# A hybrid attention and mLSTM layer: the scan stage of the last head by itself, its tiles laid out anew, stores on ScalarE's queue

## The chip, the cores and the metric

The kernel is one program on one NeuronCore of a Trainium2 chip. The time is device microseconds (us) of one execution. TensorE is called PE here, VectorE DVE, ScalarE ACT, GpSimd POOL and SyncE SP. SP computes nothing; it issues most of the DMAs, in the order in which they are written, and an issue that has to wait holds up everything behind it in that queue. ACT issues a few DMAs in the same way, between its own instructions. [...]

## The reference

One layer over 1152 tokens, 128 prompt tokens (block 0) and 1024 sample tokens (blocks 1 to 8), float32, width 1024:

```
h = rmsnorm(x) * (1 + sc1) + sh1                # adaLN from silu(cond) @ w_ada + b_ada, six parts
aq, ak, av, mq, mk, mv, mo, mg = split(h @ w_in)
attn_o = attention(rope(norm(aq)), keys, vals)  # 8 query heads of 64, 2 key heads, softmax over up to 1152 keys
hm     = mlstm_bidir(mq, mk, mv, mg)            # 4 heads of 128, chunks of 128, forward and backward scan
hm     = rmsnorm(hm) * sigmoid(mo)
x = x + g1 * (concat(attn_o, hm) @ w_out)       # w_out: 1024 x 1024
h2 = rmsnorm(x) * (1 + sc2) + sh2
x = x + g2 * ((silu(h2 @ w_g) * (h2 @ w_u)) @ w_down)   # inner width 2816
y = rmsnorm(x)
```

g1 is part 2 of the six adaLN parts, g2 part 5. The keys and values of the prompt and the scans' final states are returned too.

## The kernel before

Tokens come in nine blocks of 128 and three chunks of three blocks. Most float32 products are made of three: an operand is split into a high part (a rounded copy, by ACT) and the rest (by DVE or POOL), and high x high, high x rest and rest x high are added. `load_piece` (L139 to L153) does so for a weight: a DMA into a raw tile, ACT's copy at L152, DVE's subtraction at L137.

The program is a chain of stages. First come the projections, head by head; the scan of head h-1 and the attention of chunk 0 run beside the projection of head h. The change is in what follows:

- **The scan stage.** The scan of the last mLSTM head (`head_mlstm`, L822 to L900) has no projection beside it. For each block it makes weights (L843 to L851), products with the state (L866, L869) and with the values (L873), a sum on DVE (L876 to L884), and the block's output tile `hm` (L886 to L890). After blocks 2, 5 and 8 the last three blocks are normalised (DVE's `rsqrt`, L127 to L133, then POOL at L896) and stored to DRAM (`hm_d`, L898). Beside it run three others, advanced in turn by `weave` and `beside`: `ada`, which makes part 5 of the adaLN vector out of eight slices of w_ada (L341, L422, L441 to L454); `first`, which multiplies the attention output of chunk 0 by the upper half of w_out (`out_block`, L1148 to L1150, twelve matmuls for each block and each half of the columns, so 72), gates it (L1247) and adds it to x (POOL, L1248), storing the sums `x1a` at L1251; and `att`, the attention of chunk 1 (`attention`, L993 to L1074: scores S at L1036, softmax L1038 to L1043, two DMA transposes of the probabilities at L1045 and L1046, products with the values at L1060 and L1061).
- **The prefill** (`prefill`, L1150 to L1209). The pools of the scan stage are closed, and new pools take their memory. For each block it loads the scan's output from `hm_d` (L1162), transposes it on PE (L116), splits it (L1185 and L137), multiplies it by the lower half of w_out, and gates and adds. The loaded tile and the temporary of the gating share one tag, `t2`, with three buffers. The rows of chunk 0 are then normalised for the FFN (`norm2`). Units of `att` are put between the steps, 0.35 of one for each step.
- **The FFN** by chunks (L1316 to L1318 and L1116 to L1118), with the rest of `att` beside that of chunk 0.

Tiles of closed pools hand on their memory: the first DMA into a new tile waits for the last use of whatever lay there. The loop that begins with the tag `cs` at L527 names the tags of the pool `mlp` once, and so fixes their order in memory. The Tile framework's scheduler then orders the instructions of each engine when the program is built; `hot(n)` raises the priority of what stands under it.

Of the kernel before, what the change touches and what calls it, by code (L numbers as in the profile page):

```python
# [19 lines left out]
P = 128  # L20
# [25 lines left out]
def hybrid_step(ctx: ExitStack, tc: tile.TileContext, I: dict, O: dict):  # L46
# [11 lines left out]
    def nm(s):  # L58
        uid[0] += 1
        return f"{s}_{uid[0]}"  # L60
# [10 lines left out]
    def emit(gen):  # L71
        for _ in gen:
            pass
# [340 lines left out]
    Gv = G.rearrange("p t (d x) -> p d t x", d=2)  # L414


    def ada_rest(ns, silp, new_a4, new_part, new_row, early=2, whole=False):

        def rows_of(n, j, q, half):
            a4 = new_a4()  # L420
            lo = n * D + j * 512 + q * 256
            dma(a4, w_ada[half * 512 : half * 512 + 512, lo : lo + 256].rearrange("(k p) n -> p k n", p=P))  # L422
            return a4

        units = [(n, j, q, half) for n in ns for j in range(2) for q in range(2) for half in range(2)]
        ahead = [rows_of(*u) for u in units[:early]]
        for u, (n, j, q, half) in enumerate(units):
            if u + early < len(units):
                ahead.append(rows_of(*units[u + early]))
# [20 lines left out]
            mm(pr[0:2, :], strip_sel, part, start=True, stop=True)  # L450
# [76 lines left out]
    for tag, shape, bufs, dt in (("cs", [P, P + 1], CSB, F32), ("c0f", [P, P + 1], 2, F32), ("c0b", [P, P + 1], 1, F32), ("hm", [P, NB, P], 2, F32), ("ssh", [P, NB], 2, F32), ("nu", [P, 2, P + 1], 4, F32),  # L527
                                 ("it", [P, 2, P + 1], 3, F32), ("dn", [P, 2], 3, F32), ("jkh", [P, P], 1, BF16), ("sd", [P, 2, P], 4, F32),
                                 ("dt", [P, 2, P], 4, F32), ("so", [P, P], 9, F32), ("va", [P, P + 1], 9, F32), ("kT", [P, P], 9, F32),
                                 ("th", [P, P], 1, F32), ("qTm", [P, CT], 2 * NCH, F32), ("wv", [P, 2, P + 1], 2, F32), ("kt", [P, P], 2, F32)):  # L530
        mlp.tile(shape, dt, name=f"lay_{tag}", tag=tag, bufs=bufs)


# [565 lines left out]
    def t2():  # L1099
        return ft.tile([P, 512], F32, name=nm("t2"), tag="t2", bufs=3)  # L1100
# [20 lines left out]
            for ps, i in zip(banks, grp):  # L1121
                done(i, ps)

    def out_pieces(half, own=None):
        ws = []
        for n in range(2):
            pieces = []
            for j in range(2):
                r0 = half * 512 + 2 * j * P
                rows = w_out[r0 : r0 + 2 * P, n * 512 : (n + 1) * 512].rearrange("(a p) n -> p a n", p=P)  # L1130
                pieces.append(load_piece([(full_view, rows)], (2, 512), raw=own and own[2], own=own))
                own = None
            ws.append(pieces)
        return ws

    def out_gates():
        gs = []
# [15 lines left out]
    def prefill(cur, nxt):  # L1153

        x1s = cur["x1"], nxt["x1"]
        cur["rs"] = []

        def load_hm(b):
            if b == NB:
                return None  # L1160
            hm = t2()
            dma(hm, hm_d[b // CB][b % CB * P : (b % CB + 1) * P, :])  # L1162
# [10 lines left out]
        gx_all = xp.tile([P, D], F32, name="gx_all")  # L1173
        dma(gx_all, g_d[0, 0:1, :].to_broadcast([P, D]))
        gx = [gx_all[:, n * 512 : (n + 1) * 512] for n in range(2)]
        for b in range(NB):
            load_x1(b + 1)
            t = xp.tile([P, NQ, P], F32R, name=nm("mx"), tag="mx", bufs=2)
            th, tl = t[:, 0:4], t[:, 4:8]
            hm, ahead = ahead, load_hm(b + 1)  # L1180
# [4 lines left out]
            nc.scalar.copy(th, psv)  # L1185
            sub(tl, psv, th.bitcast(F32), "dve")
            yield
            c, i = divmod(b, CB)
            for n in range(2):
                cs = slice(n * 512, (n + 1) * 512)  # L1190
                ps = out_block(ws, n, th, tl)
                g = gx[n] if b == 0 else gs[n]
                if c < 2:
                    add_gated(x1s[c][i], ps, g, n, pool)
                else:
                    xt = t2()
                    dma(xt, xrow(b)[:, cs])
                    t = t2()
                    dve.tensor_tensor(out=t, in0=ps, in1=g, op=ALU.mult)
                    pool.tensor_tensor(out=xt, in0=xt, in1=t, op=ALU.add)  # L1200
                    dma(x1_d[i][:, cs], xt)
                yield
            if c == 0:
                with hot(200):
                    cur["rs"] += stats(x1s[0][i : i + 1])
            if 0 < b <= CB:
                yield from norm2(0, cur, b - 1)

    def attn_out_first(oT, ready):  # L1209


        x1 = hTp.tile([P, CB, D], F32, name="x1a", tag="hT0")
        gt = hTp.tile([P, 6, 512], F32, name="gta", tag="hT1")
        mx = hTp.tile([P, CB, NQ, P], F32R, name="mxa", tag="hT2")
        ip = [wp.tile([P, 1024], F32R if i < 2 else F32, name=nm("ip"), tag="ipair", bufs=4) for i in range(4)]
        ir = [wp.tile([P, 1024], F32R if i < 2 else F32, name=nm("ir"), tag="iraw", bufs=4) for i in range(4)]
        turn = [0]

        def a4():
            turn[0] += 1  # L1220
            return ip[2 + turn[0] % 2].rearrange("p (k n) -> p k n", k=4)

        ada = ada_rest((5,), padded_sil(gt[:, 5, 0:256].rearrange("p (k c) -> p k c", k=KD)), a4,
                       lambda: ir[3][:, 0:512], lambda: ir[3][0:2, 512:1024], 1)

        def out():
            for n in range(2):
                cs = slice(n * 512, (n + 1) * 512)
                ws = []
                for j in range(2):  # L1230
                    rows = w_out[2 * j * P : (2 * j + 2) * P, cs].rearrange("(a p) n -> p a n", p=P)
                    ws.append(load_piece([(full_view, rows)], (2, 512), raw=ir[2], own=(ip[j], ir[j])))
                for cnd in range(2):
                    dma(gt[:, 2 * n + cnd], g_d[0, cnd : cnd + 1, cs].to_broadcast([P, 512]))
                yield
                for i in range(CB):
# [11 lines left out]
                    pool.tensor_tensor(out=v, in0=v, in1=gt[:, 4], op=ALU.add)  # L1248
                    yield
                    if n == 1:  # L1250
                        dma(x1a_d[i], x1[:, i])  # L1251

        return out(), ada

    def attn_out(a, oT, gs):

        ws = out_pieces(0)
        x1 = a["x1"]
        for i in range(CB):
            if i != 1:  # L1260
# [178 lines left out]
    es1.close()  # L1439
    es_wp.close()  # L1440
    es_d.close()
# [10 lines left out]
    cur["x1"], nxt["x1"] = new_x1(0), new_x1(1)  # L1452
    es_x = ExitStack()
    xp = es_x.enter_context(tc.tile_pool(name="xp", bufs=1, side="right", reuse_waits="tile"))
    due = 0.0
    for _ in prefill(cur, nxt):
        due += 0.35
# [103 lines left out]
```

## Time and profile before

| | |
|---|---|
| time, three runs | 1567.03 us median (1566.90 to 1569.09) |
| the profiled execution's own time | 1570.49 us, of which the span is 1568.7 us |
| PE busy | 1486.6 us, 95% of the span |
| DVE busy | 1014.5 us, 65% |
| ACT busy | 771.1 us, 49% |
| POOL busy | 268.4 us, 17% |
| mean granted PE clock | 0.981 of full speed |

Starts and durations below are microseconds from the start of the span. In a timeline a row gives start, duration, engine, line, operation, and out<-in; `xN` is a number of merged instructions, and a bracket holds the idle time of the engine before it and who ended it. A matmul's duration includes its way through the array; the distance from one start to the next says more of its cost. In a table by windows the columns are the window, its length, and for each engine the busy time and (xN) the number of instructions, then the granted PE clock, the share of the DMA engines that was busy and the GB/s moved.

### The profile page before, as it was taken

The numbers are of one execution on the slowest core, as the hardware profiler recorded it, in microseconds if no ns is written. First come the engines' busy times: TensorE is split into PE (matmuls) and PEld (weight loads), VectorE is DVE, ScalarE is ACT, GpSimd is POOL, SyncE is SP. The second block draws the span as 40 slices with busy tenths as digits, with TensorE's granted clock in tenths as the row PEclk, the third lists the DMA queues.
The fourth block names the chain that finished last, engine by engine and source line by source line (L and its number), as shares of the span: only waits on it lengthen the run. The fifth ranks groups of instructions, "written<-read, shape, count | busy, mean of one in ns | idle before, by whom it ended". The sixth has DMA issues, their size and how long they took to land. (4 is left out here: it accounts for less than half of the span.)

```text
span 1568.7 us, 23368 instructions
## 1 busy us (share of the span) xinstructions
PE 1486.6 (95%) x8539; PEld 1246.3 (79%) x8539; DVE 1014.5 (65%) x2009; ACT 771.1 (49%) x1413; POOL 268.4 (17%) x352
## 2 busy tenths in 40 slices
PE   6899999999999589999999999999999999999997
PEld 3545567677766468898998989989898989999996
DVE  4877555837659576677555676878866585554554
ACT  4754466847656344545432444556552443323333
POOL 0212423322343242100110101000010101001110
PEclk9899999999999799999999999999999999999999
DMA  9664423523646738768554446878773545534441
GB/s 363 189 188 152 89 69 41 118 50 68 127 141 167 259 79 199 184 182 174 149 154 148 148 127 223 200 173 183 173 172 114 165 131 175 161 117 139 148 139 63
DMA packets 387881, 236.91 MB, mean 151 GB/s; under 512 B 170198, under 2 KB 346790, under 8 KB 387766
## 3 DMA queue, kind: packets, MB, share of 16 engines
q1 hardware_dynamic: 385110, 231.84, 54.8%
q10 hardware_dynamic: 2656, 3.58, 1.1%
q8 instruction: 67, 1.10, 0.3%
q14 instruction: 48, 0.39, 0.1%
HBM read 183.79 MB, written 13.26 MB: 126 GB/s over the span
## 5 line engine op out<-in xcount | busy, mean ns | idle before, releaser
L152 ACT CAST whi<-raw 128x1024 fp32r<-128x1024 f32 (+1 forms) x216 | 221.8, 1027 | 410.0 <-PE mm L1317 154.4
L137 DVE TENSOR_TENSOR wlo<-raw,whi 128x1024 fp32r<-128x1024 f32 (+1 forms) x216 | 259.4, 1201 | 205.3 <-ACT whi L152 204.9
L1317 PE MATMUL mm<-aTl,whi 128*128 128x384 f32 x1056 | 355.7, 337 | 2.7 <-DVE aTl L137 2.7
L1318 PE MATMUL mm<-aTh,wlo 128*128 128x384 f32 x1056 | 354.3, 336 | 0.0
L1316 PE MATMUL mm<-aTh,whi 128*128 128x384 f32 x1056 | 353.5, 336 | 0.0
L137 POOL TENSOR_TENSOR hl<-tn,hl 128x384 fp32r<-128x384 f32 x66 | 85.3, 1292 | 839.7 <-ACT hl L1339 764.2
L1317 PEld LDWEIGHTS mm<-aTl,whi 128*128 128x128 f32 x1056 | 198.5, 188 | 3.9 <-DVE aTl L137 3.3
L1316 PEld LDWEIGHTS mm<-aTh,whi 128*128 128x128 f32 x1056 | 198.1, 188 | 0.6
L1318 PEld LDWEIGHTS mm<-aTh,wlo 128*128 128x128 f32 x1056 | 198.4, 188 | 0.0
L1117 PE MATMUL mm<-wlo,hl 128*128 128x512 f32 x372 | 145.7, 392 | 0.0
L1116 PE MATMUL mm<-whi,hl 128*128 128x512 f32 x372 | 144.4, 392 | 0.2 <-ACT hl L1339 0.2
L1118 PE MATMUL mm<-whi,hl 128*128 128x512 f32 x372 | 143.7, 393 | 0.3 <-POOL hl L137 0.3
L483 PE MATMUL wi<-ipair,hT 128*128 128x384 f16 (+2 forms) x408 | 134.9, 333 | 3.7 <-ACT th L760 1.3
L484 PE MATMUL wi<-ipair,hT 128*128 128x384 f16 (+2 forms) x408 | 134.8, 333 | 0.0
L485 PE MATMUL wi<-ipair,hT 128*128 128x384 f16 (+2 forms) x408 | 131.3, 333 | 2.0 <-DVE hT L137 2.0
L1043 DVE SCALAR_TENSOR_TENSOR pl<-pr,st,ph 128x1152 f16<-128x1152 f32 (+1 forms) x72 | 94.6, 1314 | 34.1 <-ACT ph L1042 33.2
L1039 ACT ACTIVATE pr<-S,st 128x1152 f32<-128x1152 f32 (+1 forms) x72 | 81.4, 1130 | 34.9 <-DVE st L1038 34.5
L1038 DVE TENSOR_REDUCE st<-S 128x1 f32<-128x1152 f32 (+1 forms) x72 | 88.8, 1233 | 14.0 <-PE S L1036 13.5
L1042 ACT ACTIVATE ph<-pr,st 128x1152 f16<-128x1152 f32 (+1 forms) x72 | 83.8, 1164 | 24.0 <-issue 11.1
L1036 PE MATMUL S<-kst,qT 128*128 128x384 f32 (+1 forms) x400 | 88.2, 350 | 1.8 <-ACT pr L1039 1.8
L1105 DVE TENSOR_TENSOR t<-mm,gl 128x512 f32<-128x512 f32 x102 | 68.9, 684 | 26.7 <-DMA gl<-g_d 10.3
L1118 PEld LDWEIGHTS mm<-whi,hl 128*128 128x128 f32 x372 | 69.9, 188 | 14.9 <-POOL hl L137 0.7
(381 smaller groups left out, 2525.5 us busy)
## 6 DMA issues: line engine op xcount, KB each, us to landing
raw<-in_w_gu_dram SPq DMA_DIRECT2D x132, 512.0 KB
raw<-in_w_down_dram SPq DMA_DIRECT2D x60, 512.0 KB
a<-in_w_ada_dram SPq DMA_DIRECT2D x24, 512.0 KB
gl<-g_d SPq DMA_DIRECT2D x36, 256.0 KB
aw<-in_w_ada_dram SPq DMA_DIRECT2D x16, 512.0 KB
iraw<-in_w_in_dram SPq DMA_DIRECT2D x32, 256.0 KB
raw<-in_w_out_dram SPq DMA_DIRECT2D x12, 512.0 KB
x<-in_x_sample_dram SPq DMA_DIRECT2D x11, 512.0 KB
```

The lines of the kernel that those rows point to most:

```text
L137: (dve if eng == "dve" else pool).tensor_tensor(out=out, in0=full, in1=hi, op=ALU.subtract)
L152: nc.scalar.copy(hi[:, :n], raw[:, :n])
L483: mm(ps[:, :n], ah, wh[:, k % 2, c0 : c0 + n], start=(k == 0), stop=False)
L484: mm(ps[:, :n], ah, wl[:, k % 2, c0 : c0 + n], start=False, stop=False)
L485: mm(ps[:, :n], al, wh[:, k % 2, c0 : c0 + n], start=False, stop=(k == KD - 1))
L1043: dve.scalar_tensor_tensor(out=plv, in0=prv, scalar=st[:, 3:4], in1=phv, op0=ALU.mult, op1=ALU.subtract)
L1116: mm(ps, ah, wh[:, k % 2, :], start=(k == 0), stop=False)
L1117: mm(ps, ah, wl[:, k % 2, :], start=False, stop=False)
L1118: mm(ps, al, wh[:, k % 2, :], start=False, stop=(k == nk - 1))
L1316: mm(ps, wh[:, k, :], th[:, k, :], start=(k == 0), stop=False)
L1317: mm(ps, wh[:, k, :], tl[:, k, :], start=False, stop=False)
L1318: mm(ps, wl[:, k, :], th[:, k, :], start=False, stop=(k == KD - 1))
```

## The change

Five things, all about the scan stage and the prefill:

1. **The attention goes behind the scan stage.** `attention(0)` is finished before the stage (`emit(att)`), and `attention(1)` first runs in the prefill. The rates of the other two go up: `ada` from 0.5 to 0.8 of a step for each step of the scan, `first` from 0.35 to 0.55.
2. **Layout.** The tags of `mlp` are named in another order. `x1a` and the split attention output `mxa` change places in the memory of the projection's input; the split halves of w_out's upper half lie in the `iraw` tiles, and their raw loads have two `ipair` tiles in place of one raw tile.
3. **The gate row of `ada`** lies in the scan's second output tile (`hmx`, tag `hm`), and its stores go by ACT's queue.
4. **The stores of `x1a`** are gathered and written out after the loops, on ACT's queue.
5. **The prefill** loads the scan's output into tiles of its own (`hmr`, two buffers), has three buffers for the split, splits blocks 0 and 1 first, and makes the left halves of both before the right ones. The second half of the lower w_out, and two loads of x, are issued behind the load of the gate.

```
@@ the layout of mlp
-    for tag, ... in (("cs", ...), ("c0f", ...), ("c0b", ...), ("hm", ...), ... ("qTm", ...), ("wv", ...), ("kt", ...)):
+    for tag, ... in (("hm", ...), ("ssh", ...), ("nu", ...), ... ("kt", ...), ("wv", ...), ("c0f", ...), ("c0b", ...),
+                     ("cs", [P, P + 1], CSB, F32), ("qTm", [P, CT], 2 * NCH, F32)):
@@ ada_rest
-            dma(g_d[0 if n == 2 else 1, :, j * 512 : (j + 1) * 512], row)
+            store(g_d[0 if n == 2 else 1, :, j * 512 : (j + 1) * 512], row)
@@ prefill
-            hm = t2()
+            hm = xp.tile([P, 512], F32, name=nm("hmr"), tag="hmr", bufs=2)
...
-        ahead = load_hm(0)
-        load_x1(0)
-        ws = out_pieces(1)
+        hms = [load_hm(0), load_hm(1)]
+        ws = [out_pieces(1, 0)]
         gs = out_gates()
+        with tc.issue_after(dma(gx_all, g_d[0, 0:1, :].to_broadcast([P, D])).ins):
+            load_x1(0)
+            load_x1(1)
+            ws.append(out_pieces(1, 1))
...
+        for b in range(2):
+            mix(b)
+            yield
+        for b in range(2):
+            half(b, 0)
+            yield
+        for b in range(2):
+            load_x1(b + 2)
+            half(b, 1)
+            yield
+            yield from end(b)
+        for b in range(2, NB):
+            load_x1(b + 2)
+            mix(b)
+            yield
+            for n in range(2):
+                half(b, n)
+                yield
+            yield from end(b)
@@ attn_out_first
-        x1 = hTp.tile(..., name="x1a", tag="hT0")
-        mx = hTp.tile(..., name="mxa", tag="hT2")
+        x1 = hTp.tile(..., name="x1a", tag="hT2")
+        mx = hTp.tile(..., name="mxa", tag="hT0")
+        his, los, raws = ir[0:2], ir[2:4], ip[2:4]
+        hmx = mlp.tile([P, NB, P], F32, name="hmx", tag="hm", bufs=2).rearrange("p b n -> p (b n)")
...
-                    ws.append(load_piece([(full_view, rows)], (2, 512), raw=ir[2], own=(ip[j], ir[j])))
+                    ws.append(load_piece([(full_view, rows)], (2, 512), raw=raws[j], own=(his[j], los[j])))
...
-                        dma(x1a_d[i], x1[:, i])
+                        stores.append((x1a_d[i], x1[:, i]))
@@ the stage
-    first, ada = attn_out_first(oT, done)
+    stores = []
+    first, ada = attn_out_first(oT, done, stores)
+    emit(att)
     oT = []
-    att = chain(att, attention(1, oT, set()))
-    weave(scan, beside((ada, 0.5), (first, 0.35), (att, 0.14)), 37, 37)
-    while len(done) < CB:
-        next(att)
+    att = attention(1, oT, set())
+    weave(scan, beside((ada, 0.8), (first, 0.55)), 37, 37)
     emit(first)
     emit(ada)
     emit(scan)
+    for out, v in stores:
+        nc.scalar.dma_start(out, v)
```

What this does to the instructions of an engine is the scheduler's doing. Two places carry the prediction.

PE at the end of the scan stage, before. `mxa` is the split attention output, `ip` and `ir` are the split w_out; `S` are scores; `po` and `vs` are the attention's product with the values.

```order
L1148 MATMUL mm_6214<-ip_5710,mxa 128x512
L1149 MATMUL mm_6214<-ir_5714,mxa 128x512
L1150 MATMUL mm_6214<-ip_5710,mxa 128x512
L450 MATMUL mm_6298<-ir_5716,strip_sel 2x512
L1036 MATMUL S_6581<-kst_1029,qT_5827 128x384 x6
L1060 LDWEIGHTS vs
L1060 MATMUL po_6412<-phT_5944,vs 128x256
L1061 LDWEIGHTS vs
L1061 MATMUL po_6412<-plT_5945,vs 128x256
```

The same place of the changed kernel; `wi<-va,sd` is the scan's product with the values, `wi<-cs,qT` that with the state, `hmr` the scan's output loaded back, `whi` and `wlo` the lower half of w_out, `mx` the split `hmr`.

```order
L450 MATMUL mm_6103<-hmx,strip_sel 2x512
L874 MATMUL wi_6158<-va_5591,sd_6017 128x129 x2
L867 MATMUL wi_6172<-cs_5608,qT_4895 128x129
L867 MATMUL wi_6172<-c_905_4693,qT_4895 128x129
L874 MATMUL wi_6178<-va_5687,sd_6081 128x129 x2
L116 MATMUL mm_6284<-ident,hmr_6247 128x128 x4
L116 MATMUL mm_6294<-ident,hmr_6249 128x128 x4
L1145 MATMUL mm_6303<-whi_6252,mx_6283 128x512
L116 MATMUL mm_6322<-ident,qr_6319 128x128 x4
L1146 MATMUL mm_6303<-wlo_6253,mx_6283 128x512
L1147 MATMUL mm_6303<-whi_6252,mx_6283 128x512
```

Between the scan's last product and the prefill's first transposes stood the last twelve matmuls of `first`, one set of scores and two sets of products with the values; now nothing stands there, and the attention's first transposes (`qr`) come inside the prefill. Counted over the whole order, 40 sets of scores (one head of one block each) stood ahead of the FFN's first matmul, 33 of them ahead of the prefill's first product; now it is 35 and 27. The products with the values come in sets of 18 matmuls for two heads: ahead of the prefill's first product stand two sets fewer than before, and in the prefill four where there were three.

SP's queue before, ahead of the first load of scan output:

```order
L1045 DMA_TRANSPOSE phT_6173<-ph_6256 128x9x128
L1251 DMA x1a_d_80<-x1a 128x1024
L1046 DMA_TRANSPOSE plT_6174<-pl_6257 128x9x128
L1251 DMA x1a_d_81<-x1a 128x1024
L454 DMA g_d<-ir_5716 2x512
L1045 DMA_TRANSPOSE phT_6497<-ph_6500 128x9x128
L1046 DMA_TRANSPOSE plT_6498<-pl_6501 128x9x128
L151 DMA raw_6338<-in_w_out_dram 128x2x512
L151 DMA raw_6344<-in_w_out_dram 128x2x512
L151 DMA raw_6350<-in_w_out_dram 128x2x512
L1162 DMA t_1279_6335<-hm_d_75 128x512
```

And in the changed kernel, where the two `ip` are the last slices of w_ada for `ada`:

```order
L422 DMA ip_5710<-in_w_ada_dram 128x4x256
L422 DMA ip_5709<-in_w_ada_dram 128x4x256
L151 DMA raw_6251<-in_w_out_dram 128x2x512
L151 DMA raw_6257<-in_w_out_dram 128x2x512
L1159 DMA hmr_6247<-hm_d_75 128x512
L1159 DMA hmr_6249<-hm_d_75 128x512
L1137 DMA gl_6263<-g_d 128x512
L1137 DMA gl_6265<-g_d 128x512
L1170 DMA gx_all<-g_d 128x1024
L1164 DMA x_1250_6239<-x1a_d_79 128x1024
L1164 DMA x_1250_6239<-x1a_d_80 128x1024
L151 DMA raw_6271<-in_w_out_dram 128x2x512
```

The stores of `x1a` and of the gate row and the transposes are gone from between, two weight loads stand ahead of the first load of `hmr`, and the other two behind the load of the gate. [...]

More of the change, by code (lines that the diff above doesn't have):

```diff
@@ L414, in hybrid_step, with ada_rest @@
     Gv = G.rearrange("p t (d x) -> p d t x", d=2)
-    def ada_rest(ns, silp, new_a4, new_part, new_row, early=2, whole=False):
+    def ada_rest(ns, silp, new_a4, new_part, new_row, early=2, whole=False, store=dma):
         def rows_of(n, j, q, half):
@@ L1122, in three_blocks, with out_pieces @@
                 done(i, ps)
[L1124 to L1134, printed above, removed]
+    def out_pieces(half, n):
+        pieces = []
+        for j in range(2):
+            r0 = half * 512 + 2 * j * P
+            rows = w_out[r0 : r0 + 2 * P, n * 512 : (n + 1) * 512].rearrange("(a p) n -> p a n", p=P)
+            pieces.append(load_piece([(full_view, rows)], (2, 512)))
+        return pieces
     def out_gates():
@@ L1186, in prefill, with half @@
             sub(tl, psv, th.bitcast(F32), "dve")
-            yield
+            hms.append(load_hm(b + 2))
+        def half(b, n):
             c, i = divmod(b, CB)
[L1189 to L1202, printed above, removed]
@@ L1203, in prefill @@
-            if c == 0:
+            cs = slice(n * 512, (n + 1) * 512)
+            ps = out_block(ws, n, *mixed[b])
+            g = gx[n] if b == 0 else gs[n]
+            if c < 2:
+                add_gated(x1s[c][i], ps, g, n, pool)
+            else:
+                xt = t2()
+                dma(xt, xrow(b)[:, cs])
+                t = t2()
+                dve.tensor_tensor(out=t, in0=ps, in1=g, op=ALU.mult)
+                pool.tensor_tensor(out=xt, in0=xt, in1=t, op=ALU.add)
+                dma(x1_d[i][:, cs], xt)
@@ L1204, in prefill, with end @@
+        def end(b):
+            if b < CB:
                 with hot(200):
-                    cur["rs"] += stats(x1s[0][i : i + 1])
+                    cur["rs"] += stats(x1s[0][b : b + 1])
             if 0 < b <= CB:
                 yield from norm2(0, cur, b - 1)
-    def attn_out_first(oT, ready):
-        x1 = hTp.tile([P, CB, D], F32, name="x1a", tag="hT0")
-        gt = hTp.tile([P, 6, 512], F32, name="gta", tag="hT1")
-        mx = hTp.tile([P, CB, NQ, P], F32R, name="mxa", tag="hT2")
-        ip = [wp.tile([P, 1024], F32R if i < 2 else F32, name=nm("ip"), tag="ipair", bufs=4) for i in range(4)]
-        ir = [wp.tile([P, 1024], F32R if i < 2 else F32, name=nm("ir"), tag="iraw", bufs=4) for i in range(4)]
+        for b in range(2):
+            mix(b)
+            yield
@@ new lines, in prefill, with attn_out_first @@
+        for b in range(2):
[14 more added lines that the diff above has]
+            yield from end(b)
+    def attn_out_first(oT, ready, stores):
+        x1 = hTp.tile([P, CB, D], F32, name="x1a", tag="hT2")
+        gt = hTp.tile([P, 6, 512], F32, name="gta", tag="hT1")
+        mx = hTp.tile([P, CB, NQ, P], F32R, name="mxa", tag="hT0")
+        ip = [wp.tile([P, 1024], F32, name=nm("ip"), tag="ipair", bufs=4) for i in range(4)]
+        ir = [wp.tile([P, 1024], F32R, name=nm("ir"), tag="iraw", bufs=4) for i in range(4)]
+        his, los, raws = ir[0:2], ir[2:4], ip[2:4]
+        hmx = mlp.tile([P, NB, P], F32, name="hmx", tag="hm", bufs=2).rearrange("p b n -> p (b n)")
@@ L1250, in out @@
                     if n == 1:
-                        dma(x1a_d[i], x1[:, i])
+                        stores.append((x1a_d[i], x1[:, i]))
         return out(), ada
     def attn_out(a, oT, gs):
-        ws = out_pieces(0)
+        ws = [out_pieces(0, n) for n in range(2)]
         x1 = a["x1"]
@@ L1454, in hybrid_step @@
     xp = es_x.enter_context(tc.tile_pool(name="xp", bufs=1, side="right", reuse_waits="tile"))
+    for tag, shape, bufs, dt in (("gx_all", [P, D], 1, F32), ("hmr", [P, 512], 2, F32), ("mx", [P, NQ, P], 3, F32R)):
+        xp.tile(shape, dt, name=f"lay_{tag}", tag=tag, bufs=bufs)
     due = 0.0
```

27 lines of the change are left out of this document (13 added, 14 removed).

## The prediction

> **What bounds the kernel now.** The summary of busy time comes first: PE is busy for 95% of the span, so only a stretch where PE stands idle, or runs slowly, can give much.
>
> ```profile
> PE 1486.6 (95%) x8539; PEld 1246.3 (79%) x8539; DVE 1014.5 (65%) x2009; ACT 771.1 (49%) x1413; POOL 268.4 (17%) x352
> ```
>
> Then the table by windows, cut at the changes of work: the scan stage with its start (to 515.70), the gap ahead of the prefill's first product, the prefill, and the FFN.
>
> ```profile
> core 0: us, PE busy (x) PEld busy (x) DVE busy (x) ACT busy (x) POOL busy (x), PEclk, DMA share, GB/s
> 453.40:463.70 10.30, 7.13 (x42) 4.98 (x40) 9.02 (x31) 5.57 (x17) 4.86 (x7) 0.67 0.17 53
> 463.70:500.30 36.60, 35.33 (x227) 26.93 (x224) 30.88 (x81) 25.36 (x63) 13.60 (x13) 1.00 0.71 176
> 500.30:515.70 15.40, 11.48 (x61) 7.86 (x59) 13.47 (x38) 5.28 (x13) 5.43 (x5) 0.84 0.82 209
> 515.70:527.25 11.55, 1.29 (x5) 0.72 (x4) 4.87 (x9) 4.19 (x5) 0.82 (x1) 0.50 0.70 235
> 527.25:613.15 85.90, 73.76 (x367) 58.58 (x368) 57.91 (x118) 41.13 (x62) 32.00 (x22) 0.98 0.58 155
> 613.15:700.00 86.85, 85.39 (x485) 78.14 (x484) 58.30 (x78) 42.19 (x55) 11.15 (x8) 1.00 0.75 194
> ```
>
> The FFN is bound by PE (85.39 of 86.85). The loss is in front of it: 10.3 us of idle PE in the gap (11.55 - 1.29), 3.9 in the 15.40 before it, 12.1 in the prefill (85.90 - 73.76), and a clock of 0.50 to 0.84 around the gap. PE's timeline says what stands there:
>
> ```profile
> 500.26 0.61 PE L873 MATMUL wi<-va,sd 128*128 128x129 f32 x4
> 500.63 0.48 PE L1148 MATMUL mm<-ip,mxa 128*128 128x512 f32 x1
> 503.55 1.02 PE L450 MATMUL mm<-ir,strip_sel 128*2 128x512 f32 x2
> 506.48 0.27 PE L1060 MATMUL po<-phT,vs 128*128 128x256 f16 x1 [0.67 <-DVE gta L1247]
> 508.34 0.27 PE L1061 MATMUL po<-plT,vs 128*128 128x256 f16 x1
> 511.85 0.39 PE L1060 MATMUL po<-phT,vs 128*128 128x256 f16 x1 [3.24 <-DVE oT L1065]
> 515.45 0.42 PE L1061 MATMUL po<-plT,vs 128*128 128x256 f16 x1
> 525.46 1.12 PE L116 MATMUL mm<-ident,t 128*128 128x128 f32 x4 [9.59 <-DMA t<-hm_d]
> 527.25 0.79 PE L1148 MATMUL mm<-whi,mx 128*128 128x512 f32 x1 [0.68 <-ACT mx L1185]
> 613.15 0.33 PE L1316 MATMUL mm<-aTh,whi 128*128 128x384 f32 x1
> ```
>
> The scan's last product ends at about 500.9, and the prefill's first starts 26 us later. The wait of 9.59 us is for a load of block 0's scan output, which was stored long before; SP's queue shows why it came late.
>
> ```profile
> 511.40 1.27 SPq L1046 DMA_TRANSPOSE plT<-pl  x1
> 512.73 8.19 SPq L151 DMA_DIRECT2D raw<-in_w_out_dram  x3
> 520.96 0.47 SPq L1162 DMA_DIRECT2D t<-hm_d  x1
> ```
>
> The load stands behind a transpose of attention probabilities and behind three loads of w_out, the third of which waits until a raw buffer has been split. That split is on ACT and DVE, behind the scan's tail.
>
> **The attention behind the scan.** What leaves the stage, by the counts of the order: six sets of scores and two sets of products with the values.
>
> ```profile
> 492.90 1.31 PE L1036 MATMUL S<-kst,qT 128*128 128x384 f32 x6
> 494.04 0.61 PE L873 MATMUL wi<-va,sd 128*128 128x129 f32 x4
> ```
>
> A set of scores costs 494.04 - 492.90 = 1.14 us of PE; 18 products with the values, from 506.48 to just past 508.34, 2.0. (The four query transposes, under a microsecond, I leave out.) This is not saved, it moves: one set of scores and one of products into the prefill (1.1 + 2.0 = 3.1 us), the other five and one (5.7 + 2.0 = 7.7 us) into the FFN, at PE's full price there, since PE has no idle time to hide it. So the change breaks even when the FFN starts at 613.15 - 7.7 = 605.4.
>
> What it frees is DVE. The groups of DVE between 463.7 and 511.9, the attention's:
>
> ```profile
> L1038 DVE TENSOR_REDUCE st<-S 128x1 f32<-128x1152 f32 x6 | 8.1, 1345 | 0.9 <-PE S L1036 0.9
> L1043 DVE SCALAR_TENSOR_TENSOR pl<-pr,st,ph 128x1152 f16<-128x1152 f32 x5 | 7.0, 1403 | 0.0
> L137 DVE TENSOR_TENSOR qT<-mm,qT 64x512 fp32r<-64x512 f32 x2 | 1.4, 688 | 0.1
> L1065 DVE SCALAR_TENSOR_TENSOR oT<-po,vsc,ol 64x128 f32<-64x128 f32 x2 | 0.7, 338 | 0.0
> ```
>
> They are 17.2 us of a stretch of 48.2 in which DVE has hardly a pause. That is why the last block, whose product with the values was ready at 500.9, has its output only at 512.3:
>
> ```profile
> 504.33 0.42 DVE L876 TENSOR_TENSOR nu<-wi,it 128x258 f32<-128x258 f32 x1
> 511.83 0.47 DVE L887 SCALAR_TENSOR_TENSOR hm<-nu,dn,hm 128x128 f32<-128x128 f32 x1
> 516.47 0.70 DVE L1065 SCALAR_TENSOR_TENSOR oT<-po,vsc,ol 64x128 f32<-64x128 f32 x2 [1.81 <-ACT ol L1063]
> 518.76 0.37 ACTq L898 DMA_DIRECT2D hm_d<-hm  x1
> ```
>
> Now by engine, from 463.7. DVE has 48.2 - 17.2 = 31 us left up to that output: 494.7 at the earliest. PE has 35.33 less five sets of scores (5.7), so 29.6, and the twelve products from 500.63 with the gate row's two, up to 504.6 (503.55 + 1.02; I count 3.9): 33.5 us, so 497.2 for the scan's last product if it never waits. PE is the later. I add 1.3 us for its waits: **498.5**, estimated; the bounds are 497 and 505.
>
> The tail: from the last product to the last output tile, nu 0.42, three small DVE operations and ACT's scaling, about 1.6 us when DVE is free. From there to the store it took 518.76 - 511.83 = 6.9 us, of which 2.5 (0.70 + 1.81) were the attention's: 4.4. One split of a weight on DVE falls into it, by the page's row of such splits:
>
> ```profile
> L137 DVE TENSOR_TENSOR wlo<-raw,whi 128x1024 fp32r<-128x1024 f32 (+1 forms) x216 | 259.4, 1201 | 205.3 <-ACT whi L152 204.9
> ```
>
> That is 1.2 us. ACT splits `hmr` only behind that store (0.7, by the 0.68 that PE waited for it at 527.25). 498.5 + 1.6 + 4.4 + 1.2 + 0.7 = 506.4, say **507** for the prefill's first product, where 527.25 was. Bounds: 6.5 to 9 us behind the last product.
>
> **Layout, loads, gate row.** The two first w_out loads now wait only for the seventh w_ada slice and the splitting, both well inside the scan, and no transpose stands ahead of them. I cost them, and the first `hmr` loads, at nothing: the tail above covers them. [...] The second half of w_out waits for the last scan store and is needed two half blocks later, so two times twelve matmuls, 5.8 us at the 0.24 of those from 500.63 to 503.55; that may stall PE by 0 to 3 us, which is in the prefill's idle time below. At the stage's start both raw tiles of w_out's upper half are loaded behind the last projection; before, one piece was:
>
> ```profile
> 453.04 1.04 ACT L152 CAST ip<-ir 128x1024 fp32r<-128x1024 f32 x1 [0.46 <-DMA ir<-in_w_out_dram]
> ```
>
> That was late by 0.46 us already. Two loads instead of one behind two others: between 1 us better and 2 us worse; I take 0.
>
> **Stores on ACT's queue.** Three stores of `x1a` and two of the gate row now wait in ACT's order for POOL and DVE; queued behind them are the scan's scalings and squares, for which DVE waits.
>
> ```profile
> SPq L1251 <- POOL x1a L1248: 5.3, 3, 3.4
> 503.09 2.46 POOL L1248 TENSOR_TENSOR x1a<-x1a,gta 128x512 f32<-128x512 f32 x1 [2.95 <-DVE rt L132]
> ```
>
> SP waited 5.3 us for POOL there. On ACT the same wait costs between 0 (POOL done by then) and 5.3; I take 0 with the 1.3 above, since POOL is busy for 13.60 of 36.60. [...]
>
> **The prefill.** Its PE work is 73.76 + 3.1 = 76.9 us. Its idle time was 12.1; of it this much was the split of `hmr`, which now runs ahead:
>
> ```profile
> PE mm L1148 <- ACT mx L1185: 4.6, 5, 1.6
> ```
>
> One of those five (0.68) lies before the prefill. So 12.1 - 3.9 = 8.2 if nothing comes instead, 14 if the late w_out half and the moved attention add to it; I take 10. The FFN starts at 507 + 76.9 + 10 = 593.9, against 605.4: **11.5 us gained.** Against the execution's own 1570.49 that is 1559.0; against the median of 1567.03, **1555.5**.
>
> **The rivals.**
> *Early:* PE never waits (497.2), a tail of 6.5, idle 8.2: the FFN at 588.8, 16.6 us gained, 1550; less still if parts overlap.
> *ACT held:* the stores take their 5.3 us from the scan: 6.2 us gained, 1561.
> *Nothing comes of it:* the gate, `x1a` and the second half of w_out hang on stores that are issued last, 505 + 9 and idle 14: 604.9, 0.5 us gained, 1566.5.
> *Slower, a cold PE:* taking matmuls out of the stage lets PE's clock fall.
>
> ```profile
> 491.07 0.47 PE L1148 MATMUL mm<-ip,mxa 128*128 128x512 f32 x1 [1.21 <-DVE sd L851]
> 529.12 0.63 PE L1150 MATMUL mm<-whi,mx 128*128 128x512 f32 x1
> 529.55 0.63 PE L1148 MATMUL mm<-whi,mx 128*128 128x512 f32 x1
> ```
>
> After the gap one matmul followed the other by 0.43 us (529.12 to 529.55); the twelve from 500.63 to 503.55 took 0.24 each, so the price is 1.8 times as high. After the pause of 3.24 us the products with the values took 0.42 each, not 0.27; after 1.21 nothing happened. With all 33.5 us of the stage's work at 1.8 times the price, 60, the last product comes at 463.7 + 60 + 1.3 = 525, the prefill's first at 533.5, and the FFN, 86.9 later, at 620.4: 15 us slower than 605.4, **1582**. It decides against the change once the stage's end is 11.5 us late, from 14 us of work done cold (14 x 0.8), so from several pauses of about 3 us. Against it: with an idle time of 1 to 8 us in the whole stage there is room for one. [...]
> *Slower, the FFN pays twice:* ten more transposes in SP's queue between the loads of w_gu. At 1.3 us each, as above, that is 13 us, and loads late by all of it would leave 1.5 us of loss, 1568.5. Against it: transposes stand there already, and PE was idle for 1.5 us.
>
> **How the numbers follow.** A run tells 0.2%, 3.1 us, from no change. Forecast 0.55, early 0.08, ACT held 0.13: all faster, 0.76. Nothing comes of it 0.09, the FFN pays twice 0.04: together 0.13, of which 0.11 within 0.2% and 0.02 slower. A cold PE 0.11: slower, so 0.13 in all. The range runs from beyond the early case, 1547, to the end of the fourth, 1567; it leaves out a little of the early case and what is slower.
>
> **What would show it.** Right: no S rows between 463 and 500; the scan's last product near 498.5; the wait for the load of scan output gone or under 3 us; the prefill's first product at 503 to 514; the FFN's first matmul at 589 to 600; DVE busy by some 17 us less there. Wrong: an FFN start behind 605; ACT idle on a store ahead of the scan's scalings; a clock under 0.9 between 464 and 500; new waits for w_gu in the FFN.

## The result: 4.9 us faster, where 11.5 were forecast

| | before | changed |
|---|---|---|
| time, seven runs each | 1569.09 us median (1566.90 to 1571.23) | 1564.23 us median (1562.19 to 1566.24) |
| ratio | | 0.997, 95% interval 0.9958 to 0.9982 |
| the profiled execution | 1570.49, span 1568.7 | 1563.28, span 1561.5 |

The change is faster, by 0.3% where 0.73% was forecast, and 1564.23 lies inside the range. The two profiled executions differ by 7.2 us, 2.3 more than the medians: that of before took 1.4 us more than its median, that of the changed kernel 1.0 less. What is read from one profile against the other is therefore some 2 us too good.

Busy times hardly differ from before. From the page of the changed kernel:

```profile
PE 1484.1 (95%) x8539; PEld 1251.8 (80%) x8539; DVE 1017.1 (65%) x2009; ACT 772.3 (49%) x1413; POOL 264.9 (17%) x352
```

The table by windows of the changed kernel, cut at its own changes of work: the scan stage, the gap, the prefill's first 16 us, a second gap, the rest of the prefill to the FFN's first matmul, and the FFN.

```profile
core 0: us, PE busy (x) PEld busy (x) DVE busy (x) ACT busy (x) POOL busy (x), PEclk, DMA share, GB/s
463.70:500.30 36.60, 36.12 (x228) 26.02 (x227) 28.62 (x89) 15.82 (x52) 15.75 (x16) 0.96 0.59 184
500.30:508.94 8.64, 0.80 (x7) 0.42 (x5) 5.78 (x22) 4.03 (x10) 2.79 (x4) 0.74 0.85 293
508.94:525.06 16.12, 16.12 (x63) 13.44 (x64) 9.75 (x13) 6.27 (x8) 3.50 (x2) 0.82 0.87 304
525.06:533.41 8.35, 0.40 (x2) 0.00 (x0) 6.94 (x28) 4.12 (x7) 3.46 (x2) 0.69 0.74 185
533.41:597.42 64.01, 60.02 (x308) 50.23 (x309) 44.19 (x84) 33.69 (x51) 25.00 (x17) 0.91 0.55 114
597.42:686.00 88.58, 87.97 (x496) 82.23 (x494) 60.53 (x82) 44.99 (x57) 11.59 (x9) 1.00 0.76 191
```

The gap of before (11.55 us with 1.29 of work) has shrunk to 8.64 us with 0.80. But there is a second one now, 8.35 us with 0.40 of work, in the middle of the prefill. PE's timeline gives the points that the prediction named, and the new one:

```profile
499.29 0.71 PE L874 MATMUL wi<-va,sd 128*128 128x129 f32 x4 [0.46 <-DVE nu L877]
501.14 0.66 PE L116 MATMUL mm<-ident,hmr 128*128 128x128 f32 x4 [0.70 <-DMA hmr<-hm_d]
508.94 0.80 PE L1145 MATMUL mm<-whi,mx 128*128 128x512 f32 x1 [7.14 <-ACT mx L1185]
525.07 0.40 PE L1147 MATMUL mm<-whi,mx 128*128 128x512 f32 x1
533.41 1.97 PE L116 MATMUL mm<-ident,y 128*128 128x128 f32 x8 [7.95 <-ACT y L1319]
597.42 0.33 PE L1340 MATMUL mm<-aTh,whi 128*128 128x384 f32 x1
603.68 0.39 PE L1147 MATMUL mm<-whi,mx 128*128 128x512 f32 x1
```

The scan's last product (forecast 498.5) is at 499.29, the load of scan output is waited for 0.70 us (9.59 before), and the prefill's first product (forecast 507) is at 508.94. The FFN's first matmul (forecast 593.9) is at 597.42, but that row flatters: 20 products of the prefill stand behind it, up to 603.68. At 0.23 us each they are 4.6 us, so the FFN has in truth begun at 597.42 + 4.6 = 602.0, 8.1 us behind the forecast. From there to the end of the span it is 1561.5 - 602.0 = 959.5 us; before it was 1568.7 - 613.15 = 955.6.

Against the forecast the prefill's first product is 1.9 us late, the prefill is 6.2 us longer (93.1 us from 508.94 to 602.0, where 86.9 were forecast), and the rest is 3.8 us shorter than the 955.6 + 7.7 that I had. That leaves 4.3 us, by which this execution misses its forecast of 1559.0. The other 2.3 us of the 6.6 between 11.5 and 4.9 are the distance of the two profiled executions from their medians.

**The second gap.** y is a block's normalised row for the FFN (`norm2`). The chain to it begins with the last product of block 0 and runs over DVE, POOL and ACT. The timeline of the changed kernel on these three:

```profile
524.46 1.41 DVE L1044 SCALAR_TENSOR_TENSOR pl<-pr,st,ph 128x1152 f16<-128x1152 f32 x1
525.78 0.68 DVE L1106 TENSOR_TENSOR t<-mm,gx_all 128x512 f32<-128x512 f32 x1
526.54 3.46 POOL L1107 TENSOR_TENSOR x<-x,t 128x512 f32<-128x512 f32 x2 [3.62 <-DVE t L1106]
527.84 1.06 ACT L1303 ACTIVATE jk<-x 128x1024 bf16<-128x1024 f32 x1 [1.26 <-POOL x L1107]
529.02 0.15 DVE L127 TENSOR_SCALAR rv<-s 128x1 f32<-128x1 f32 x1
531.22 0.15 DVE L127 TENSOR_SCALAR rv<-s 128x1 f32<-128x1 f32 x1 [1.00 <-ACT jk L1303]
532.45 0.16 DVE L133 SCALAR_TENSOR_TENSOR ry<-rt,ry 128x1 f32<-128x1 f32 x1
532.64 1.33 ACT L1319 ACTIVATE y<-x,ry 128x512 f32<-128x512 f32 x2 [1.45 <-DVE ry L133]
```

Gate (525.78), addition (526.54), sum of squares (527.84), root (529.02 to 532.6), scaling (532.64): from 525.5 to 533.4 PE has nothing to do. Two delays in the chain come of what runs beside it. The gate starts only behind a softmax step of the moved attention (524.46), and the root of block 0 stands for 1.00 us until ACT has the sum of squares of block 1 (531.22), since DVE's order puts the beginning of block 1's root into the middle of block 0's. From the start of block 0's last product, at 523.91, to the transposes of y it takes 9.5 us. In sum the chain was about as long before, 8.7 us: there the last product of block 0 started at 534.51 and the transposes of y at 543.24. But between them PE made the 24 products of block 1, and waited for `y` for only 1.49 us. Now the order of PE has this (`mm_6348` is the right half of block 0, `mm_6384` that of block 1):

```
4098 L1146 MATMUL mm_6348<-wlo_6279,mx_6283 128x512
4099 L1147 MATMUL mm_6348<-whi_6278,mx_6283 128x512
4100 L1145 MATMUL mm_6348<-whi_6278,mx_6283 128x512
4101 L1146 MATMUL mm_6348<-wlo_6279,mx_6283 128x512
4102 L1147 MATMUL mm_6348<-whi_6278,mx_6283 128x512
4103 L1146 MATMUL mm_6384<-wlo_6279,mx_6293 128x512
4104 L1147 MATMUL mm_6384<-whi_6278,mx_6293 128x512
4105 L1145 MATMUL mm_6384<-whi_6278,mx_6293 128x512
4106 L1146 MATMUL mm_6384<-wlo_6279,mx_6293 128x512
4107 L1147 MATMUL mm_6384<-whi_6278,mx_6293 128x512
4108 L116 MATMUL mm_6445<-ident,y_6443 128x128 x4
```

Both blocks are split ahead, the second half of w_out comes last, and both right halves end together: five products, 1.2 us, stand between block 0's last product and y.

**The clock behind it.** The windows around the gap:

```profile
528.30:533.41 5.11, 0.00 (x0) 0.00 (x0) 3.70 (x25) 2.61 (x6) 1.71 (x1) 0.50 0.44 122
533.41:542.00 8.59, 7.94 (x29) 6.79 (x30) 5.69 (x12) 6.61 (x12) 2.56 (x2) 0.50 0.21 51
542.00:553.00 11.00, 11.00 (x63) 9.17 (x63) 9.10 (x18) 6.85 (x12) 6.16 (x4) 1.00 0.76 108
```

Sets of scores in and behind that stretch, from PE's timeline:

```profile
536.88 2.29 PE L1037 MATMUL S<-kst,qT 128*128 128x384 f32 x6 [0.65 <-ACT pr L1040]
555.75 1.22 PE L1037 MATMUL S<-kst,qT 128*128 128x384 f32 x6
```

The granted clock is 0.50 from 528.3 to 542.0, for 8.6 us after PE has work again; a set of scores takes 2.29 us there, 1.22 later. 7.94 us of work at half the clock are an estimated 4 us lost beside the 7.95 of the gap. That is more than the 6.2 us by which the prefill is too long, because the forecast had 10 us of idle PE in the prefill. The rest of its idle time is only 4.0 us (64.01 - 60.02).

**At the stage's start.** ACT and PE of the changed kernel, where the last projection ends:

```profile
450.11 1.04 ACT L152 CAST ir<-ip 128x1024 fp32r<-128x1024 f32 x1 [3.38 <-DMA ip<-in_w_out_dram]
452.35 0.33 PE L116 MATMUL mm<-ident,kt 128*128 128x128 f32 x1 [3.46 <-ACT it L870]
```

ACT stands at the split of w_out for 3.38 us, until its load has landed; the scan's scaling `it` is queued behind it, and PE waits for that.

### The profile page after: what moved, and what is told of

It is laid out like the page before. It is cut to its first block, busy times and chain, and to the rows that moved or that the text cites. A ratio compares the mean times of both kernels' runs of the same rounds, so it can differ in the third digit from the quotient of the medians.

```text
span 1561.5 us, 23390 instructions
## 1 busy us (share of the span) xinstructions
PE 1484.1 (95%) x8539; PEld 1251.8 (80%) x8539; DVE 1017.1 (65%) x2009; ACT 772.3 (49%) x1413; POOL 264.9 (17%) x352
## 4 chain that ended last, share of the span: by engine, by line
PE 58%; DVE 3%; DMA 1%; ACT 1%; issue 0%; POOL 0%; ACTq 0%; DVEq 0%
PE mm L1341 11%; PE mm L1342 11%; PE mm L1340 11%; PE mm L1117 5%; PE mm L1118 5%; PE mm L1119 5%; PE S L1037 3%; PE po L1062 2%; PE po L1061 1%; PE mm L1145 1%; PE mm L1146 1%; PE mm L1147 1%; DVE wlo L137 1%; DMA raw<-in_w_gu_dram 1%; DVE fl L1329 1%; DVE t L1106 1%
```

## The experiments

Theory P: the shortfall is the second gap with its slow clock, and in a smaller part the load at the stage's start. Rival Q: the moved attention is dear wherever it lies, and the gap is only where that shows.

**The norm one block later** (changed kernel):

```
-            if 0 < b <= CB:
-                yield from norm2(0, cur, b - 1)
+            if 1 < b <= CB + 1:
+                yield from norm2(0, cur, b - 2)
```

> The changed kernel, but the prefill transposes block b-2 for the FFN behind block b, not block b-1. Theory P (the shortfall is the pause of 7.95 us in the prefill, where PE has come to the transposes of the FFN's input before their statistics are there, and the half clock for 8.8 us behind it): pause and half clock go, 8 to 12 us faster than the changed kernel, 1552 to 1556. Theory Q (the moved attention is dear wherever it lies: its softmax on DVE and ACT holds up the prefill, the pause is only where it shows): the pause comes back at a later place, within 2 us of the changed kernel.

Measured: 1555.31 us, ratio to before 0.9917 (0.9902 to 0.9932), so 0.53% or 8 us better than the change itself. Its PE timeline, then the window of its prefill:

```profile
510.16 0.79 PE L1145 MATMUL mm<-whi,mx 128*128 128x512 f32 x1 [7.85 <-ACT mx L1185]
536.65 0.39 PE L1062 MATMUL po<-plT,vs 128*128 128x256 f16 x1 [3.00 <-DMA plT<-pl]
539.97 1.04 PE L116 MATMUL mm<-ident,y 128*128 128x128 f32 x8
592.92 0.33 PE L1340 MATMUL mm<-aTh,whi 128*128 128x384 f32 x1
```

```profile
510.16:592.92 82.76, 75.91 (x375) 62.05 (x376) 62.00 (x125) 44.80 (x66) 35.66 (x23) 0.95 0.67 172
```

y is not waited for at all, the clock of the prefill is 0.95, and it takes 82.76 us; no product of it stands behind the FFN's first matmul. All eight sets of scores that the changed kernel has in its prefill are still in it (48 matmuls), and three of the four sets of products with the values, so Q falls. Here the forecast sum can be read without the flaw: the FFN starts 613.15 - 592.92 = 20.2 us earlier (forecast 19.25), and the rest takes 960.7 us, 5.1 more than before (forecast 7.7), the fourth set of products (2.0 us) with it.

**w_out's raw tiles** in the spare iraw tiles (changed kernel):

```
-        ip = [wp.tile([P, 1024], F32, name=nm("ip"), tag="ipair", bufs=4) for i in range(4)]
-        ir = [wp.tile([P, 1024], F32R, name=nm("ir"), tag="iraw", bufs=4) for i in range(4)]
+        ip = [wp.tile([P, 1024], F32R if i < 2 else F32, name=nm("ip"), tag="ipair", bufs=4) for i in range(4)]
+        ir = [wp.tile([P, 1024], F32R if i < 2 else F32, name=nm("ir"), tag="iraw", bufs=4) for i in range(4)]
-        his, los, raws = ir[0:2], ir[2:4], ip[2:4]
+        his, los, raws = ip[0:2], ir[0:2], ir[2:4]
...
-            return ip[turn[0] % 2].rearrange("p (k n) -> p k n", k=4)
+            return ip[2 + turn[0] % 2].rearrange("p (k n) -> p k n", k=4)
```

> The changed kernel, but the raw loads of w_out's upper half go into the two spare iraw tiles, not into the ipair tiles of the last projection, as far as the memory is free earlier. If ACT's wait of 3.38 us for that load, ahead of the scan's scaling, is on the path that sets the end: 2 to 4 us faster than the changed kernel, 1560 to 1562, with PE's pause of 3.46 us at the stage's start under 1 us. If the stage catches up anyway (PE or DVE is late by as much later on): within 1 us.

Measured: 1559.59 us, 0.9952 (0.9938 to 0.9965), 0.18% or 3 us better than the change; the two intervals overlap a little. Its PE timeline:

```profile
449.97 0.33 PE L116 MATMUL mm<-ident,kt 128*128 128x128 f32 x1 [0.32 <-ACT it L870]
454.30 0.67 PE L786 MATMUL mm<-wv,kt 128*128 128x258 f32 x2 [1.41 <-ACT cs L797]
494.45 0.71 PE L874 MATMUL wi<-va,sd 128*128 128x129 f32 x4
506.42 0.79 PE L1145 MATMUL mm<-whi,mx 128*128 128x512 f32 x1 [5.62 <-ACT mx L1185]
```

The 3.46 us are now 0.32 and, for the second piece, 1.41, and between these two waits the products with the values follow one another by 0.11 us (450.65 to 452.51). In the changed kernel it is 0.21 us each behind the 3.46 of waiting (454.11 to 456.24), and the granted clock from 445.0 to 463.7 is 0.90. The scan's last product is 4.8 us earlier (494.45), the prefill's first only 2.5 (506.42). So by the trace the load was on the path, and my price of 0, with 2 us as the worst, was too low; that the time gains by it is likely, not certain.

**The attention back beside the scan** (changed kernel; its edit stands below), and **the attention's move alone** (kernel before, with the reverse of this edit). Both have the higher rates of `ada` and `first`:

```
-    emit(att)
     oT = []
-    att = attention(1, oT, set())
-    weave(scan, beside((ada, 0.8), (first, 0.55)), 37, 37)
+    att = chain(att, attention(1, oT, set()))
+    weave(scan, beside((ada, 0.8), (first, 0.55), (att, 0.14)), 37, 37)
+    while len(done) < CB:
+        next(att)
```

> The changed kernel with the attention of chunk 1 put back beside the scan (0.14 of a unit for each step of the scan). The prediction's step (it frees 17 us of DVE in the stage and costs some 8 us of PE in prefill and FFN): the scan's last product 8 to 13 us later than at 499.3, the rest 6 to 10 us shorter; 1 to 5 us slower than the changed kernel, 1565 to 1569. Theory Q: 3 us or more faster than the changed kernel.

> The kernel before with nothing but part 1: the attention behind the scan and the two higher rates. Theory P: the scan ends 8 to 13 us earlier, the FFN is some 8 us longer, and the old prefill has no pause of 7.95 us: 1 to 6 us faster than before, 1563 to 1568. Theory Q: slower than before by 2 us or more.

Measured: 1576.25 us, 1.0057 (1.0043 to 1.0072), for the first, slower than before and 0.87%, 13.6 us, slower than the change: outside what I expected. And 1566.51, 0.9994 (0.9982 to 1.0006), for the second: no gain that can be told. PE and SP of the first of them, then the same of the second, whose profiled execution (1571.36) was the slowest of its twelve:

```profile
512.25 0.37 PE L1061 MATMUL po<-phT,vs 128*128 128x256 f16 x1 [4.13 <-ACT pr L1040]
523.32 1.94 PE L116 MATMUL mm<-ident,hmr 128*128 128x128 f32 x8 [6.57 <-DMA hmr<-hm_d]
518.96 1.31 SPq L1047 DMA_TRANSPOSE plT<-pl  x1
520.36 1.07 SPq L1159 DMA_DIRECT2D hmr<-hm_d  x2
```

```profile
499.69 0.71 PE L873 MATMUL wi<-va,sd 128*128 128x129 f32 x4 [0.77 <-DVE nu L876]
515.85 1.09 PE L116 MATMUL mm<-ident,t 128*128 128x128 f32 x4 [15.45 <-DMA t<-hm_d]
500.60 8.12 SPq L151 DMA_DIRECT2D raw<-in_w_out_dram  x4
608.21 0.33 PE L1316 MATMUL mm<-aTh,whi 128*128 128x384 f32 x1
```

In the first, the scan's last product is at 507.51, 8.2 us later than in the changed kernel, as I had expected. What I had not expected stands behind it. The loads of `hmr` are again queued behind transposes of the attention, PE waits for them 6.57 us, and the prefill's first product comes only at 525.08: 17.6 us behind the scan's last, where the changed kernel has 9.65. The prefill is as long as there (93.4 us, its last 20 products counted as above), and the rest shorter by 2.6 us, where I had expected 6 to 10. So of the 13.9 us between the two profiled executions 8.2 are the scan stage and 7.9 the way from it into the prefill. How much of this the higher rates make, which before did not have, no run shows.

The second shows why the parts need each other. The scan ends as early as in the changed kernel (499.69), but the old prefill's load of its output stands behind four loads of w_out (8.12 us in SP's queue), and PE waits for 15.45 us where it was 9.59. The FFN starts 4.9 us earlier, and pays 1569.6 - 608.21 = 961.4 us against 955.6: nothing is left. So 13.6 us hang on the move with the new prefill around it, and none that can be told without it.

**Both edits that helped, together.**

> The changed kernel with both edits that helped: w_out's raw tiles in iraw, and the norm for the FFN one block later. If the two losses lie one behind the other and don't hide each other: 13.0 us faster than before by the later norm and 2 to 4 by the load, 1551 to 1554 where before is 1567, ratio 0.989 to 0.991. If the earlier stage only makes a longer wait for the loads in the prefill: no better than the later norm alone, 0.992.

Measured: 1558.35 us, 0.9936 (0.9923 to 0.9948): no better than the later norm alone (0.9917; the intervals overlap a little). PE:

```profile
508.97 0.80 PE L1145 MATMUL mm<-whi,mx 128*128 128x512 f32 x1 [6.91 <-ACT mx L1185]
538.03 1.12 PE L116 MATMUL mm<-ident,y 128*128 128x128 f32 x4 [3.36 <-ACT y L1319]
```

The scan's last product was at 497.03, 3.5 us earlier than with the later norm alone (500.52), but the prefill's first only 1.2, and 3.36 us of waiting for y are back. I took these for the cause, and put the norm **two blocks later**.

> The two edits together (w_out's raw tiles in iraw, the FFN's norm later), the norm now two blocks later than in the changed kernel, not one. If the two did not add up because the earlier stage left the norm's chain too little cover again (3.36 us of waiting for y there): that wait goes, 1551 to 1555, ratio 0.989 to 0.992. If the earlier stage only runs into the loads of the prefill: as with one block later, 0.9936.

Measured: 1559.85 us, 0.996 (0.9945 to 0.9974). The wait for y is gone, and another one stands there; the theory of the returned wait falls:

```profile
536.42 0.79 PE L1147 MATMUL mm<-whi,mx 128*128 128x512 f32 x1 [3.01 <-DVE mx L137]
```

Why the earlier stage doesn't add up with the later norm is not settled. That 3.5 us at the scan's end become 1.2 at the prefill's start is measured. The prefill then takes 86.0 us in the first of the two (with the 20 products that here, too, stand behind the FFN's first matmul) and 86.1 in the second, against 82.76 with the later norm alone. What it loses there is not one wait: PE is idle for 9.7 and 7.8 us against 6.85, and busy for 76.4 and 78.3 against 75.9.

**The stores on SP's queue** (changed kernel; the stores of `x1a` and of the gate row issued by `nc.sync` again).

> The changed kernel with part 4 undone for the queue: the stores of x1a and of the gate row go by SP's queue, ahead of the w_out and scan output loads. The prediction's step (nothing is held on ACT, the stores are worth 0): within 2 us of the changed kernel. Rival, ACT held: 2 to 5 us faster, with the scan's last product earlier. Rival the other way: the first loads for the prefill stand behind the stores, its first product 1 to 4 us later than 508.94, as much slower.

Measured: 1565.13 us, 0.9981 (0.9971 to 0.9992), against 0.997: not told apart. PE:

```profile
505.84 1.94 PE L116 MATMUL mm<-ident,hmr 128*128 128x128 f32 x8 [6.48 <-DMA hmr<-hm_d]
509.36 0.80 PE L1145 MATMUL mm<-whi,mx 128*128 128x512 f32 x1 [1.58 <-ACT mx L1185]
```

The load of `hmr` does come 6.48 us late behind the stores, and the first product all the same at 509.36 (508.94): what PE waits for last is the split (1.58 us), which in the changed kernel stands on ACT behind the last store of the scan (issued at 507.88, the split at 508.30).

**Block by block** (changed kernel; both halves of block 0 ahead of both of block 1).

> The changed kernel with one part of part 5 undone: both halves of block 0, then both halves of block 1, where it makes the left halves of both first. If the distance between the last product of block 0 and the transposes of its normalised rows makes the pause (24 products then, 12 now): the pause of 7.95 us falls to some 4, a wait for the second half of w_out comes ahead of it (block 0's right half is due some 3 us earlier); in sum 0 to 3 us faster than the changed kernel. If the late second half of w_out makes it: no change.

Measured: 1564.05 us, 0.9972 (0.9958 to 0.9986): no change. The gap is there as before:

```profile
533.82 1.97 PE L116 MATMUL mm<-ident,y 128*128 128x128 f32 x8 [6.99 <-ACT y L1317]
```

The order in which the source makes the halves is not what counts: with both blocks split ahead, the scheduler again puts the products with the last of the weights at the end, for both blocks in turn, and again five of block 1 follow block 0's last. So this run could not test more cover for the chain. "No change" is what I expected if the late weights make the gap, and the trace fits that. But that they make it is argued, not shown.

**The later norm in the kernel before.**

> The kernel before with the norm for the FFN one block later. A control: if the later norm repairs only what the change brought, its waits for the normalised rows there (1.49 and 1.84 us) are all there is to gain: 0 to 3 us faster than before, 1564 to 1567. If it would have helped any version: 8 us or more.

Measured: 1565.28 us, 0.9983 (0.9973 to 0.9993), 2.7 us (1.1 to 4.2 by the interval). So of the 8 us that the later norm gives the changed kernel, some 3 were to be had before as well, and some 5 repair what the change brought.

**The first splits on DVE** (later norm; the high parts of blocks 0 and 1 by `dve.tensor_copy`, not behind the last store on ACT).

> The later norm alone, with the high parts of blocks 0 and 1 of the scan's output made by DVE, not by ACT behind the last scan store. If that store on ACT makes the prefill's first product late (7.85 us from the last transposes to it): the first product comes 1 to 3 us earlier, and the kernel is as much faster than the later norm alone, ratio 0.990 to 0.991. If DVE's own queue (the scan's square roots and two weight splits) holds it as long: no change, 0.992.

Measured: 1554.97 us, 0.9918 (0.9904 to 0.9933), as the later norm alone. From the scan's last product to the prefill's first it is 506.06 - 497.44 = 8.62 us, against 9.64; too little to be told in the time:

```profile
497.44 0.71 PE L874 MATMUL wi<-va,sd 128*128 128x129 f32 x4 [0.45 <-DVE nu L877]
506.06 0.77 PE L1145 MATMUL mm<-whi,mx 128*128 128x512 f32 x1 [6.57 <-DVE mx L1186]
```

The best versions are this one and the later norm alone, both 0.8% faster than before.

## Why the prediction was right in direction and too high in size

- **The attention behind the scan: right, its number in part by luck.** No scores lie between 463 and 500, the last scan product came 0.8 us behind the forecast, and taking the move back, with the higher rates left, costs 13.6 us. But that product came so near 498.5 with 3.46 us of waiting at the stage's start that I had put at 0. With half of that wait, in the run with the raw tiles in iraw, it came at 494.45, ahead of the 497.2 that I had as the earliest. That DVE would be busy by 17 us less there was wrong as a test: from 463.7 to 511.9 it was 36.3 us, not 42.3. Among what has moved up into the room are splits of w_out, of `hmr` and of the queries (4.5 us) and the scan's last square root.
- **Its price in the FFN: too high.** 7.7 us forecast; 3.9 (959.5 - 955.6) in the changed kernel, 5.1 with the later norm, 5.8 with the move alone, each from one profile. A part of that is my count: the prefill had 36 matmuls of scores before, six sets and not seven, and has 48 now. So two sets went into the prefill and four into the FFN, 4.3 and 6.6 us where I had 3.1 and 7.7. The forecast gain is the same by both, as the 1.1 us come off one term and go onto the other.
- **The tail: 9.65 us** (499.29 to 508.94) where I had 8.5 and a bound of 9. ACT's split behind the last store of the scan is the wait, as I had said; 7.14 us of it.
- **The layout: wrong.** I took 0 for the two loads behind the last projection, from the 0.46 us by which one such load had been late. I bounded the lateness, but did not ask what is queued behind the split on ACT: the scan's scaling, so 3.38 us of load became 3.46 of PE. Giving the raw tiles other memory moved the scan's end up by 4.8 us and the kernel's by some 3, with intervals that overlap a little.
- **The stores on ACT's queue: right at 0**, by the run with the stores on SP's queue (0.9981 against 0.997, not told apart).
- **The prefill: the step that failed.** "12.1 - 3.9 = 8.2 if nothing comes instead ...; I take 10": I took the wait for the split of `hmr` away and did not ask what is late next, and I gave its work no price for a slower clock. To 602.0 the prefill took 93.1 us where I had 86.9. Two blocks made in parallel end together, and the chain of some 9 us from a block's last product to its normalised row, which the products of block 1 had covered, was bare. PE was idle for 11.9 us, 7.95 of them in this one gap, so the 10 was nearly met, but by a wait that I had not thought of. The work was 81.1 us where I had 76.9: 1.1 of the difference is the second set of scores, and the rest is no more than the estimated 4 us that the half clock behind the gap cost. With the norm one block later the gap is gone and the FFN starts at 592.92, where 593.9 was forecast.
- **The rivals.** None of mine was this one. The cold PE came near: its mechanism appeared, a clock of 0.50 behind a pause, but in the prefill and through a pause of 7.95 us, while the clock between 463.7 and 500.3 was 0.96. The FFN's start of my case "early" (588.8) was met only with the later norm and the first splits on DVE (588.60, in the fastest of its runs).

## What to carry to other kernels

When work is moved or run ahead, follow not only the engine that is freed but each long chain that the old order had covered: count the instructions between the chain's first input and its consumer on the busiest engine, in the order before and after, and add the slow clock behind a pause to its price (0.50 for 5.7 and 8.6 us in the changed kernel). When a load is made later or larger, look at what stands behind its first reader in that engine's queue, not at the load's lateness alone. And parts of a change may be worth nothing singly: here the freed DVE counted for nothing while the load of the scan's output stood behind the loads of w_out in one queue.

## What the runs showed of the hardware

A pause of 7 to 8 us cost more than itself, both times in the changed kernel, because full speed came back late: with work again from 508.94, the clock was 0.50 up to 514.60, and with work again from 533.41 up to 542.00, with one gap of 0.65 us in it.

```profile
508.90:514.60 5.70, 5.66 (x15) 4.57 (x16) 2.66 (x4) 1.63 (x3) 0.00 (x0) 0.50 0.57 151
514.60:525.06 10.46, 10.46 (x49) 8.88 (x48) 7.11 (x9) 4.68 (x5) 3.50 (x2) 1.00 1.03 388
```

The way back to full speed took 5.7 us the first time and 8.6 the second; why the second took longer is not shown here. From these two a pause of 8 us costs an estimated 11 to 12 us (7.95, and half of 5.7 to 8.6).
